# First MLP product of a two-layer trunk kernel by one level of Strassen's algorithm

## The chip, the cores and the metric

The kernel runs on one core of a Trainium2 chip. The metric is the device time of one execution in microseconds. The core has a matrix engine (TensorE, PE in the profile; its weight loads are shown apart as PEld), a vector engine (VectorE, DVE), an engine for activations and copies (ScalarE, ACT), GpSimd (POOL), and SyncE (SP), whose queue issues most of the weight loads by DMA.

## The reference

A trunk of two layers over 512 latent tokens and 256 context tokens of width 1024. Each layer ends with a squared-ReLU MLP. In the names of the kernel:

```
u  = modulate(rms_norm(x), shift, scale)   # 1024 features of each token
ff = u @ w_ff1                             # 1024 x 4096
h  = relu(ff) ** 2
x  = x + gate * (h @ w_ff2)                # 4096 x 1024
```

`shift`, `scale` and `gate` belong to six modulation vectors of each layer, which come from the conditioning vector (latent tokens) or from a learned constant (context tokens). Layer 0 computes all 768 tokens. In layer 1 the result needs the 512 latent ones alone behind the attention stage, so its MLP has 512 tokens. All arithmetic is float32.

## The kernel before, in words

**Numbers.** A float32 product is made of three passes (`PASSES`): each operand is kept as a rounded part and a residue (`uh`/`ul` for the input, `whi`/`wlo` for weights, `hh`/`hl` for the hidden values), and hi·hi, hi·lo and lo·hi are added in PSUM. A weight block of 512 KB comes by DMA into a buffer with the tag `raw` (three of them); ACT casts the rounded part (L158) and DVE subtracts it for the residue (L159), in `split_raw`. Features lie on the 128 partitions, so the 1024 inputs are 8 slices and the 4096 hidden features are 32 chunks of 128; tokens run along the free dimension.

**The MLP** (`mlp`, L1072). The 32 chunks are 8 groups of 4. `ff1(f)` computes the chunks of group f: `dense` (L180, matmul L186) runs 8 slices by 3 passes, each as one matmul of 512 latent columns and, in layer 0, one of 256 context columns, because a matmul writes at most 512 columns here. `act2` (L1075) squares the relu on ACT, rounds it on DVE (L1081) and subtracts for the residue (L1082). The first three chunks of a layer are computed by `First` (L440), slice by slice, as the normalised input becomes ready. `ff2(f)` (L1096) adds the group's part of the second product for the 8 output slices and puts it on x with DVE (`gated_add`, L408). The order is ff1(0), ff1(1), ff2(0), ff1(2), ff2(1) and so on.

**Modulation vectors.** Vectors 0 and 1 of layer 0 are computed at the start, vectors 2 to 4 by `mod_vec` (L242) as matmuls on PE in the attention stage of layer 0. Vector 5 of layer 0 and all six of layer 1 are dot products on DVE beside layer 0's stages up to the end of its MLP (`mod_dot`, L280; L289 is the product, with the weight block, named modw, in a `raw` buffer too).

**What sets the order.** The program is written as generators that yield costs; `weave` mixes those that fill (table `PACE`) with the main one, and a scheduler then sets each engine's order of instructions. Tiles come from pools of a few buffers with the same tag (`u`, `z`, `aw`, `lx`, `ls`, `raw`), and whoever wants a buffer waits for its last reader.

## Time and profile before

| | us |
|---|---|
| three runs | 1634.98, 1635.94, 1640.08 (median 1635.94) |
| the profiled execution | 1638.57 |
| its span | 1635.9 |
| PE busy | 1590.0 (97% of the span), 9202 matmuls |
| PEld busy | 1334.4 (82%) |
| DVE busy | 1075.0 (66%) |
| ACT busy | 584.2 (36%) |
| POOL busy | 63.7 (4%) |
| matmuls of `ff` (L186) on the chain that ended last | 51% of the span |

The span runs from the first to the last instruction that the profiler recorded; the execution's own time is 2.7 us longer. In the chain that ended last, PE has 82% of the span, DVE 2%, ACT 1%. The profile's name `ff` stands for the outputs of both MLP products (`ff1` and `ff2` in the program). The MLP of layer 0 runs from about 460 to 960 us, that of layer 1 from about 1283 to 1625. Matmuls are pipelined: the time of one record is longer than the distance between two, so distances are read from starts. The mean granted clock of the execution was 0.986 of full speed.

### The profile page before, as it was taken

How to read it: one execution, taken by the hardware profiler on the slowest of the kernel's cores; microseconds unless marked ns; L12 is line 12 of the kernel's file. 1: busy time of each engine (PE TensorE's matmuls, PEld its weight loads, DVE VectorE, ACT ScalarE, POOL GpSimd, SP SyncE). 2: the span in 40 equal slices, each digit the busy share in tenths (PEclk: the TensorE clock that was granted, in tenths of full speed). 3: DMA queues.
4: the chain of work that ended last, by engine and by line, in shares of the span. 5: the costliest groups of instructions: out<-in, count | busy, mean ns of one | idle time of the engine just before them, and what ended most of it. 6: DMA issues, size and time to landing. Idle time of an engine off the chain costs nothing.

```text
span 1635.9 us, 23128 instructions
## 1 busy us (share of the span) xinstructions
PE 1590.0 (97%) x9202; PEld 1334.4 (82%) x9202; DVE 1075.0 (66%) x2122; ACT 584.2 (36%) x878; POOL 63.7 (4%) x106
## 2 busy tenths in 40 slices
PE   7988999999999999999999998999999999999997
PEld 3666898789888888888888886888789888888887
DVE  3785576876897676666666487966878644444447
ACT  3462223544442212122122146623655422223223
POOL 1201010000000000000000001101000000000000
PEclk8999999999999999999999999999999999999998
DMA  9347220101354343334333231222102322232233
GB/s 314 114 148 226 86 73 33 65 14 63 106 159 140 115 141 116 115 117 128 125 122 116 78 116 40 78 82 78 65 27 90 104 97 96 90 103 91 91 103 103
DMA packets 58587, 170.48 MB, mean 104 GB/s; under 512 B 6720, under 2 KB 19776, under 8 KB 58480
## 3 DMA queue, kind: packets, MB, share of 16 engines
q1 hardware_dynamic: 55216, 161.26, 30.4%
q0 software_dynamic: 2112, 6.70, 1.4%
q8 instruction: 72, 1.18, 0.3%
q10 hardware_dynamic: 1152, 1.05, 0.2%
q14 instruction: 35, 0.29, 0.1%
HBM read 165.44 MB, written 2.15 MB: 102 GB/s over the span
## 4 chain that ended last, share of the span: by engine, by line
PE 82%; DVE 2%; issue 2%; ACT 1%; POOL 0%; DMA 0%; POOLq 0%; DVEq 0%; ACTq 0%
PE ff L186 51%; PE inp L186 6%; PE outp L186 6%; PE first L440 3%; PE py L178 2%; PE S L998 2%; PE kvp L178 2%; PE pT L1020 2%; PE pn L841 1%; PE S L1000 1%; PE S L1002 1%; PE qrp L186 1%; PE sT L818 1%; PE pi L829 1%; PE lrup L608 1%
## 5 line engine op out<-in xcount | busy, mean ns | idle before, releaser
L158 ACT CAST whi<-raw 128x1024 fp32r<-128x1024 f32 x191 | 200.7, 1051 | 716.2 <-PE ff L186 571.4
L159 DVE TENSOR_TENSOR wlo<-raw,whi 128x1024 fp32r<-128x1024 f32 x191 | 233.2, 1221 | 155.8 <-ACT whi L158 151.4
L186 PE MATMUL ff<-hh,whi 128*128 128x512 f32 (+1 forms) x800 | 242.2, 348 | 0.0
L186 PE MATMUL ff<-hl,whi 128*128 128x512 f32 (+1 forms) x800 | 242.0, 348 | 0.0
L186 PE MATMUL ff<-hh,wlo 128*128 128x512 f32 (+1 forms) x800 | 241.9, 348 | 0.0
L289 DVE SCALAR_TENSOR_TENSOR modjunk<-modw,cb 128x512 f32<-128x512 f32 x224 | 154.7, 691 | 108.6 <-DMA modw<-in_w_modT 103.4
L186 PE MATMUL ff<-uh,whi 128*128 128x512 f32 (+1 forms) x696 | 210.9, 357 | 1.0 <-ACT hrelu L1077 1.0
L186 PE MATMUL ff<-uh,wlo 128*128 128x512 f32 (+1 forms) x696 | 210.2, 356 | 0.0
L186 PE MATMUL ff<-ul,whi 128*128 128x512 f32 (+1 forms) x696 | 209.4, 355 | 0.0
L408 DVE SCALAR_TENSOR_TENSOR x<-ff,mod,x 128x256 f32<-128x256 f32 (+1 forms) x200 | 123.1, 639 | 102.6 <-PE ff L186 102.5
L186 PEld LDWEIGHTS ff<-hl,whi 128*128 128x128 f32 x800 | 150.4, 188 | 20.8
L186 PEld LDWEIGHTS ff<-hh,wlo 128*128 128x128 f32 x800 | 150.3, 188 | 20.6
L186 PEld LDWEIGHTS ff<-hh,whi 128*128 128x128 f32 x800 | 150.3, 188 | 20.5
L186 PEld LDWEIGHTS ff<-uh,whi 128*128 128x128 f32 x696 | 130.8, 188 | 21.8 <-ACT hrelu L1077 1.7
L186 PEld LDWEIGHTS ff<-uh,wlo 128*128 128x128 f32 x696 | 131.0, 188 | 20.6 <-DVE wlo L159 0.5
L186 PEld LDWEIGHTS ff<-ul,whi 128*128 128x128 f32 x696 | 130.7, 188 | 20.5
L186 PE MATMUL inp<-uh,whi 128*128 128x256 f32 (+1 forms) x224 | 71.1, 374 | 2.5 <-ACT whi L158 2.5
L186 PE MATMUL inp<-uh,wlo 128*128 128x256 f32 (+1 forms) x224 | 68.3, 362 | 0.6 <-DVE wlo L159 0.6
L186 PE MATMUL inp<-ul,whi 128*128 128x256 f32 (+1 forms) x224 | 68.3, 362 | 0.0
L193 POOL TENSOR_TENSOR rsq<-rsv,nhalf 128x2 f32<-128x2 f32 (+2 forms) x16 | 14.2, 886 | 1295.8 <-DVE rsv L223 1294.4
L178 PE MATMUL kvp<-whi,uh 128*128 128x256 f32 x192 | 60.2, 313 | 4.2 <-ACT sig L613 2.9
L440 PE MATMUL first<-uh,wlo 128*128 128x256 f32 (+3 forms) x192 | 62.4, 328 | 0.6 <-DVE wlo L159 0.6
(316 smaller groups left out, 2766.2 us busy)
## 6 DMA issues: line engine op xcount, KB each, us to landing
raw<-in_w_ff2c SPq DMA_DIRECT2D x72, 512.0 KB, 3.5
raw<-in_w_ff1c SPq DMA_DIRECT2D x64, 512.0 KB, 3.4
modw<-in_w_modT SPq DMA_DIRECT2D x56, 512.0 KB, 3.9
modw<-in_w_mod SPq DMA_DIRECT2D x24, 512.0 KB, 4.2
raw<-in_w_outc SPq DMA_DIRECT2D x24, 512.0 KB, 3.4
raw<-in_w_inc SPq DMA_DIRECT2D x21, 512.0 KB, 3.5
modw<-in_w_mod SPq DMA_DIRECT2D x32, 256.0 KB, 5.2
raw<-in_w_inkv SPq DMA_DIRECT2D x8, 512.0 KB, 3.5
```

The lines of the kernel that those rows point to most:

```text
L158: nc.scalar.copy(hi, raw)
L159: V.tensor_tensor(lo, raw, hi.bitcast(F32), op=OP.subtract)
L178: mm(dst, w[a], r[b], start=first and i == 0, stop=last and i == 2)
L186: mm(ps[:M, po + t0:po + t1], wk[k][a], rk[k][b][:, t0:t1], start=(k == 0 and i == 0), stop=(k == n - 1 and i == 2))
L289: V.scalar_tensor_tensor(junk, w[:, 512 * i:512 * i + 512], 1.0, rows[2 * r + i], op0=OP.mult, op1=OP.mult, accum_out=acc[:, m, i, r:r + 1])
L408: V.scalar_tensor_tensor(x[m][:, s[0]:s[1]], ps[:, po + s[0]:po + s[1]], modv[l][:, v, m, r:r + 1], x[m][:, s[0]:s[1]], op0=OP.mult, op1=O ...
L440: mm(ps[:M, PO + s[0]:PO + s[1]], wk[k][a][:, :M], self.rk[k][b][:, s[0]:s[1]], start=(k == 0 and i == 0), stop=(k == NK - 1 and i == 2))
L608: mm(ps[:, PO + a:PO + b], wl[:, g, d, c], xs[:, a:b], start=True, stop=True)
L818: mm(sT[h][:, PO + 128 * b:PO + 128 * b + 128], kT[p][hp, bs], z["q"][p][hp, bs], start=True, stop=True)
L829: mm(pi[:, 130 * (b - a):130 * (b - a) + 130], z["q"][p][hp, 128 * b:128 * b + 128], C[p][hp, b], start=True, stop=True)
L998: mm(S[:, PO + a:PO + e], z["qk"][h][wa][:, qs], ckv[ra][:, a:e], start=(i == 0), stop=False)
L1020: nc.tensor.transpose(pt[:, PO + 128 * k:PO + 128 * k + 128], pr[:, 128 * k:128 * k + 128], ident)
```

## The change

The first group of each layer (chunks 0 to 3) is computed as before. The other 28 chunks are taken in 14 pairs. For a pair, the weight is a matrix of 2 by 2 blocks, A11 to A22 (chunk by half of the inputs, that is 4 slices), and the input is one of 2 by 2 blocks, B11 to B22 (half of the inputs by half of the tokens: 384 in layer 0, 256 in layer 1). Strassen's form (Winograd's variant) makes the 2 by 2 output blocks with seven block products in place of eight. A block product is 4 slices by 3 passes, 12 matmuls, all at one line, L1168.

- `combine` (L1106 of the changed file) makes the four input sums for each of 4 slice pairs, once a layer: `u` is put together from its two parts (L1111), four subtractions (L1116), and each result is split into a rounded part (ACT, L1119) and a residue (DVE, L1120).
- `pair` (L1154) makes the weight sums on DVE (L1187, L1188, L1191, L1200), splits each operand of 4 slices (`Halves.of`: ACT L1148, DVE L1149), and adds the products: partly in PSUM, partly through copies by ACT (L1182, L1194, L1198) and additions by DVE (L1185, L1199, L1208). Square and cast of the hidden values are ACT's now (`squares`, L1172 to L1176), the residue is DVE's (L1177).
- The second product is `down` (L1213), with the same matmuls as `ff2` had. The order is written out: four products of a pair, then the second product of the group before in between the last three, then the next pair.
- Vector 5 of layer 0 moves from `mod_dot` to `mod_vec` (PE). `mod_dot` leaves out the context row of vectors 2 to 5 of layer 1, whose context is not needed: 128 products in place of 224.
- `raw` has four buffers in place of three; the cos, sin and mask tables, `nd`, `vw` and `modst` share seven slots of a new tag `t`, and the tables are loaded once a layer; the sums of the inputs take slots `t`, `lx`, `ls` and `z`.

```diff
-        def ff1(f):
-            hs = []
-            if f == 0:
...
-            for i in range(len(hs), FB):
-                w = wchunks(split_raw(ins["w_ff1c"][l, f * FB + i], [128, NK, 128]))
-                ps = ps2("ff1")
-                yield from dense(ps, w, u, segs)
-                hs.append(act2(f, ps))
-            h[f] = hs
...
+        def combine(k, tags):
+
+            sums = []
+            for c in (k, KH + k):
+                t = slot("aw", "usum")
+                V.tensor_tensor(t[:, late], u[c][0][:, late].bitcast(F32), u[c][1][:, late].bitcast(F32), op=OP.add)
+                sums.append(t)
+            a, b = sums
+            for o, i0, i1 in ((a[:, n1], a[:, n2], a[:, n1]), (a[:, n2], b[:, n2], a[:, n2]),
+                              (b[:, n2], b[:, n2], a[:, n1]), (b[:, n1], b[:, n1], b[:, n2])):
+                V.tensor_tensor(o, i0, i1, op=OP.subtract)
+
+            def split(src, hl):
+                nc.scalar.copy(hl[0], src)
+                V.tensor_tensor(hl[1], src, hl[0].bitcast(F32), op=OP.subtract)
+                return hl
+            wide = [slot(next(tags), "t42", F32R) for _ in range(2)]
+            split(b[:, late], [t[:, late] for t in wide])
...
+            split(a[:, n2], t3)
...
+            return lambda: split(a[:, n1], t1)
...
+            def of(self, src):
+                if self.n % 2 == 0:
+                    self.hl = [wp.tile([128, 2, KH, 128], F32R, tag=t, name=t) for t in ("whi", "wlo")]
+                hi, lo = [t[:, self.n % 2] for t in self.hl]
+                self.n += 1
+                nc.scalar.copy(hi, src)
+                V.tensor_tensor(lo, src, hi.bitcast(F32), op=OP.subtract)
+                return hi, lo
...
+            def product(dst, w, name, first, last):
+                hl = halves.of(w)
+                for k in range(KH):
+                    for i, (a, b) in enumerate(PASSES):
+                        mm(dst, hl[a][:, k], right[k][name][b], start=first and k == 0 and i == 0,
+                           stop=last and k == KH - 1 and i == 2, skip_group_check=True)
+                return KH * 1.3e-3 * hN
...
+            def squares(t, done):
+
+                act(t[:, late], t[:, late], AF.Square)
+                hi, lo = slot("z", "hh", F32R), slot("lx" if done % 2 else "ls", "hl", F32R)
+                nc.scalar.copy(hi[:, late], t[:, late])
+                V.tensor_tensor(lo[:, late], t[:, late], hi[:, late].bitcast(F32), op=OP.subtract)
+                return hi, lo
+
+            cost = product(X, a11, "b11", True, False)
+            ta = slot("aw", "hrelu")
+            nc.scalar.copy(ta[:, n1], X)
+            yield cost
+            cost = product(Y, a12, "b21", True, True)
+            V.tensor_tensor(ta[:, n1], ta[:, n1], Y, op=OP.add)
+            s3 = wp.tile([128, KH, 128], F32, tag="s3", bufs=1, name="s3")
+            V.tensor_tensor(s3, a11, a21, op=OP.subtract)
+            V.tensor_tensor(a21, a21, a22, op=OP.add)
+            yield cost
+            cost = product(Z, a21, "t1", True, False)
+            V.tensor_tensor(a11, a21, a11, op=OP.subtract)
+            yield cost
+            cost = product(X, a11, "t2", False, False)
+            nc.scalar.copy(ta[:, n2], X)
+            yield cost
+            cost = product(X, s3, "t3", False, False)
+            tb = slot("aw", "hrelu")
+            nc.scalar.copy(tb[:, n2], X)
+            V.tensor_tensor(tb[:, n2], tb[:, n2], Z, op=OP.add)
+            V.tensor_tensor(a12, a12, a11, op=OP.subtract)
+            yield cost
+            cost = product(X, a22, "t4", False, True)
+            act(tb[:, n2], tb[:, n2], AF.Relu)
+            act(tb[:, n1], X, AF.Relu)
+            h[c + 1] = squares(tb, 1)
+            yield cost
+            cost = product(Z, a12, "b22", False, True)
+            V.tensor_tensor(ta[:, n2], ta[:, n2], Z, op=OP.add)
+            act(ta[:, late], ta[:, late], AF.Relu)
+            h[c] = squares(ta, 0)
+            yield cost
...
+        h = {}
+        tags = iter(TAGS[l])
+        yield from first_group()
+        h.update(enumerate(h.pop(0)))
+        todo = [combine(k, tags) for k in range(KH)]
+        for f in todo:
+            f()
+        G = NF // FB
+        one = pair(FB)
+        yield from steps(one, 4)
+        for f in range(1, G):
+
+            units, two = [], pair(f * FB + 2)
+            g = down(f - 1, [segs], units)
+            for i in range(3):
+                yield from chunks(g, units, i + 1)
+                yield from steps(one, 1)
+            if f < G - 1:
+                yield from chunks(g, units, NK + 1)
+                yield from steps(two, 4)
+                one = pair((f + 1) * FB)
+                for i in range(3):
+                    yield from chain(steps(one, 1), steps(two, 1))
+                yield from steps(one, 1)
...
+        yield from down(G - 1, sweeps, None)
...
-        filler = chain(*[mod_vec(0, v, PACE["mod"][0]) for v in range(2, 5)]) if l == 0 else None
...
+        filler = chain(*[mod_vec(0, v, PACE["mod"][0]) for v in range(2, 6)]) if l == 0 else None
```

**Where the order changes, first place: DVE behind the first group of layer 0's MLP.** Before, DVE has there the casts and residues of the squared chunks (`hh`, `hl`), residues of weights (`wlo`), and modulation products (`modjunk`):

```order
L1081 CAST hh_4294<-hrelu_4291 128x768
L289 SCALAR_TENSOR_TENSOR modjunk_4184,modacc_4232<-modw_4423,cb_4181 128x512
L1082 TENSOR_TENSOR hl_4295<-hrelu_4291,hh_4294 128x768
L1081 CAST hh_4301<-hrelu_4298 128x768
L159 TENSOR_TENSOR wlo_4389<-raw_4386,whi_4388 128x1024
L1082 TENSOR_TENSOR hl_4302<-hrelu_4298,hh_4301 128x768
L1081 CAST hh_4308<-hrelu_4305 128x768
L289 SCALAR_TENSOR_TENSOR modjunk_4184,modacc_4232<-modw_4423,cb_4182 128x512
L1082 TENSOR_TENSOR hl_4309<-hrelu_4305,hh_4308 128x768
L289 SCALAR_TENSOR_TENSOR modjunk_4184,modacc_4232<-modw_4423,cb_4183 128x512
L159 TENSOR_TENSOR wlo_4457<-raw_4454,whi_4456 128x1024
```

Now the sums of the inputs stand there. `usum` is a sum of the two parts of an input slice or a difference of such; `ul`, `t42` and `t3` are residues of the sums; `raw_4511` and `raw_4513` are the two weight blocks of the first pair. The first rows, from the first cast on:

```order
L1084 CAST hh_4356<-hrelu_4353 128x768
L1085 TENSOR_TENSOR hl_4357<-hrelu_4353,hh_4356 128x768
L1084 CAST hh_4363<-hrelu_4360 128x768
L292 SCALAR_TENSOR_TENSOR modjunk_4401,modacc_4293<-modw_4399,cb_4238 128x512
L1085 TENSOR_TENSOR hl_4364<-hrelu_4360,hh_4363 128x768
L1084 CAST hh_4370<-hrelu_4367 128x768
L292 SCALAR_TENSOR_TENSOR modjunk_4401,modacc_4293<-modw_4399,cb_4239 128x512
L1085 TENSOR_TENSOR hl_4371<-hrelu_4367,hh_4370 128x768
L292 SCALAR_TENSOR_TENSOR modjunk_4401,modacc_4293<-modw_4399,cb_4240 128x512
L1149 TENSOR_TENSOR wlo_4518<-raw_4511,whi_4517 128x512
L292 SCALAR_TENSOR_TENSOR modjunk_4401,modacc_4293<-modw_4399,cb_4241 128x512
L1111 TENSOR_TENSOR usum_4443<-uh_3962,ul_3963 128x768
```

and the last ones ahead of the weight of the third product (`wlo_4561`), with those just behind it:

```order
L1120 TENSOR_TENSOR t3_4486<-usum_4489,t3_4485 128x384
L1116 TENSOR_TENSOR usum_4491<-usum_4491 128x384
L292 SCALAR_TENSOR_TENSOR modjunk_4537,modacc_4293<-modw_4535,cb_4238 128x512
L1149 TENSOR_TENSOR wlo_4561<-raw_4513,whi_4560 128x512
L1120 TENSOR_TENSOR t42_4498<-usum_4491,t42_4497 128x768
L292 SCALAR_TENSOR_TENSOR modjunk_4537,modacc_4293<-modw_4535,cb_4239 128x512
L1185 TENSOR_TENSOR hrelu_4533<-hrelu_4533,str_4515 128x384
L292 SCALAR_TENSOR_TENSOR modjunk_4537,modacc_4293<-modw_4535,cb_4240 128x512
L1191 TENSOR_TENSOR raw_4511<-raw_4513,raw_4511 128x512
L292 SCALAR_TENSOR_TENSOR modjunk_4537,modacc_4293<-modw_4535,cb_4241 128x512
L159 TENSOR_TENSOR wlo_4595<-raw_4592,whi_4594 128x1024
```

Between these two pieces are 35 more rows, nearly all of `combine`; the residue of the third product's weight is the 51st operation from the cast `hh_4356` on.

**Second place: PE at the same point.** Before, the matmuls of one chunk follow those of another, with the same inputs:

```order
L186 MATMUL ff1_4318<-ul_3919,whi_4314 128x256
L186 MATMUL ff1_4318<-ul_3919,whi_4314 128x512
L186 MATMUL ff1_4318<-uh_3918,wlo_4315 128x256
L186 MATMUL ff1_4318<-uh_3918,wlo_4315 128x512
L186 MATMUL ff1_4392<-uh_3904,whi_4388 128x256
L186 MATMUL ff1_4392<-uh_3904,whi_4388 128x512
L186 MATMUL ff1_4392<-ul_3905,whi_4388 128x256
L186 MATMUL ff1_4392<-ul_3905,whi_4388 128x512
```

Now the first two products of the pair write `str_4515`; behind the first one, the start of the third (`strq_4516`, with `whi_4560`) and eight matmuls of the second MLP product are put:

```order
L1168 MATMUL str_4515<-uh_3968,wlo_4518 128x384
L1168 MATMUL strq_4516<-uh_3962,whi_4560 128x384
L186 MATMUL ff2_4598<-hh_4356,whi_4594 128x256
L186 MATMUL ff2_4598<-hh_4356,whi_4594 128x512
L186 MATMUL ff2_4598<-hl_4357,whi_4594 128x256
L186 MATMUL ff2_4598<-hl_4357,whi_4594 128x512
L186 MATMUL ff2_4632<-hh_4356,whi_4594 128x256
L186 MATMUL ff2_4632<-hh_4356,whi_4594 128x512
L186 MATMUL ff2_4632<-hl_4357,whi_4594 128x256
L186 MATMUL ff2_4632<-hl_4357,whi_4594 128x512
L1168 MATMUL strq_4516<-ul_3963,whi_4560 128x384
L1168 MATMUL str_4515<-uh_3970,whi_4517 128x384
```

and behind the second product the rest of the third, which reads `ul_3963` and `wlo_4561` (the residues in the lists of DVE above) and is followed by all others of the pair:

```order
L1168 MATMUL str_4515<-uh_3976,wlo_4518 128x384
L1168 MATMUL strq_4516<-uh_3962,wlo_4561 128x384
L1168 MATMUL strq_4516<-uh_3964,whi_4560 128x384
L1168 MATMUL strq_4516<-ul_3965,whi_4560 128x384
L1168 MATMUL strq_4516<-uh_3964,wlo_4561 128x384
```

The third product reads the tile of slice 0 whose second half of tokens DVE and ACT have written over with a sum.

**Third place: the head of a later group in layer 0.** SP's queue of loads there (modw: modulation weights; `in_w_ff1c` and `in_w_ff2c`: weights of the two MLP products), before:

```order
L155 DMA raw_5067<-in_w_ff1c 128x1024
L286 DMA modw_5092<-in_w_modT 128x1024
L155 DMA raw_5135<-in_w_ff1c 128x1024
L286 DMA modw_5160<-in_w_modT 128x1024
L155 DMA raw_5203<-in_w_ff2c 128x1024
L155 DMA raw_5265<-in_w_ff2c 128x1024
L286 DMA modw_5285<-in_w_modT 128x1024
```

and now; `raw_5733` is the first weight block of the second product in its group, and its buffer is the one that `modw_5647` had:

```order
L1159 DMA raw_5587<-in_w_ff1c 128x1024
L1159 DMA raw_5589<-in_w_ff1c 128x1024
L288 DMA modw_5647<-in_w_modT 128x1024
L288 DMA modw_5728<-in_w_modT 128x1024
L155 DMA raw_5733<-in_w_ff2c 128x1024
L288 DMA modw_5773<-in_w_modT 128x1024
L155 DMA raw_5818<-in_w_ff2c 128x1024
```

DVE at that place now (`hrelu` additions are those of product results, `hl` residues of hidden values):

```order
L1199 TENSOR_TENSOR hrelu_5625<-hrelu_5625,strq_5512 128x384
L1185 TENSOR_TENSOR hrelu_5607<-hrelu_5607,str_5591 128x384
L1177 TENSOR_TENSOR hl_5672<-hrelu_5625,hh_5671 128x768
L292 SCALAR_TENSOR_TENSOR modjunk_5649,modacc_5581<-modw_5647,cb_4238 128x512
L292 SCALAR_TENSOR_TENSOR modjunk_5649,modacc_5581<-modw_5647,cb_4239 128x512
L1208 TENSOR_TENSOR hrelu_5527<-hrelu_5527,strq_5512 128x384
L292 SCALAR_TENSOR_TENSOR modjunk_5730,modacc_5581<-modw_5728,cb_4238 128x512
L292 SCALAR_TENSOR_TENSOR modjunk_5730,modacc_5581<-modw_5728,cb_4239 128x512
L1177 TENSOR_TENSOR hl_5710<-hrelu_5527,hh_5709 128x768
L159 TENSOR_TENSOR wlo_5736<-raw_5733,whi_5735 128x1024
```

Before, the loads of the second product came one behind another, and each pair of modulation products stood between splits; now a modulation load comes ahead of the first of them, and its two products stand behind the residue `hl_5672`, ahead of `wlo_5736`.

## Rows read from the trace of the kernel before

**Rows 1.** Windows: stretch, length, busy us (count) of PE, PEld, DVE, ACT, POOL, clock, DMA, GB/s.
```profile
460.00:960.00 500.00, 499.77 (x2879) 437.86 (x2878) 338.53 (x702) 121.05 (x139) 0.66 (x1) 1.00 0.38 125
1283.00:1625.00 342.00, 340.93 (x1568) 280.66 (x1568) 167.85 (x221) 108.09 (x144) 0.70 (x1) 1.00 0.30 98
```

**Rows 2.** Timeline of PE, layer 0's MLP; columns: start, us, instruction; eleven passes apart.
```profile
599.88 0.51 PE L186 MATMUL ff<-hh,wlo 128*128 128x256 f32 x2
...
603.71 0.51 PE L186 MATMUL ff<-ul,whi 128*128 128x256 f32 x2
```

**Rows 3.** Timeline of PE, layer 1's MLP, eighteen matmuls apart.
```profile
1399.67 0.39 PE L186 MATMUL ff<-uh,wlo 128*128 128x512 f32 x1
...
1403.84 0.39 PE L186 MATMUL ff<-hh,wlo 128*128 128x512 f32 x1
```

**Rows 4.** Timeline of PE, last second product of layer 1, 73 matmuls apart.
```profile
1600.39 0.28 PE L186 MATMUL ff<-hh,whi 128*128 128x256 f32 x1
...
1609.06 0.29 PE L186 MATMUL ff<-hl,whi 128*128 128x256 f32 x1
```

**Rows 5.** Groups by form, PE: busy us, mean ns, idle before.
```profile
L186 PE MATMUL ff<-hh,whi 128*128 128x512 f32 x480 | 188.9, 394 | 0.0
...
L186 PE MATMUL ff<-hh,whi 128*128 128x256 f32 x320 | 89.6, 280 | 0.0
```

**Rows 6.** Groups by form, DVE.
```profile
L289 DVE SCALAR_TENSOR_TENSOR modjunk<-modw,cb 128x512 f32<-128x512 f32 x224 | 154.7, 691 | 108.6 <-DMA modw<-in_w_modT 103.4
...
L1082 DVE TENSOR_TENSOR hl<-hrelu,hh 128x768 fp32r<-128x768 f32 x32 | 30.6, 957 | 0.8
...
L1082 DVE TENSOR_TENSOR hl<-hrelu,hh 128x512 fp32r<-128x512 f32 x32 | 22.2, 693 | 1.1
...
L213 DVE TENSOR_TENSOR n1acc<-n1acc,n1sq 128x256 f32<-128x256 f32 x21 | 8.8, 418 | 0.1
```

**Rows 7.** Timeline of DVE ahead of and behind the first group of layer 0.
```profile
442.75 0.74 DVE L337 SCALAR_TENSOR_TENSOR xn<-x,mod,nps 128x512 f32<-128x512 f32 x1
...
445.40 2.06 DVE L337 SCALAR_TENSOR_TENSOR xn<-x,mod,nps 128x512 f32<-128x512 f32 x3
...
462.10 0.56 DVE L1081 CAST hh<-hrelu 128x768 fp32r<-128x768 f32 x1
```

**Rows 8.** Timeline of ACT at the end of chunk 3, layers 0 and 1; idle before.
```profile
469.38 0.81 ACT L1077 ACTIVATE hrelu<-ff 128x768 f32<-128x768 f32 x1 [3.27 <-PE ff L186]
...
1289.50 1.05 ACT L158 CAST whi<-raw 128x1024 fp32r<-128x1024 f32 x1 [1.56 <-PE ff L186]
```

**Rows 9.** Timeline of DVE, first cast of layer 1's MLP.
```profile
1284.56 0.43 DVE L1081 CAST hh<-hrelu 128x512 fp32r<-128x512 f32 x1 [0.28 <-ACT hrelu L1078]
```

**Rows 10.** Windows of 1 and 2 us where PE was idle.
```profile
102.00:103.00 1.00, 0.27 (x3) 0.07 (x1) 1.00 (x1) 0.00 (x0) 0.00 (x0) 1.00 0.07 29
...
106.00:107.00 1.00, 0.74 (x6) 0.41 (x10) 1.00 (x4) 0.00 (x0) 0.00 (x0) 0.50 0.00 0
...
110.00:111.00 1.00, 1.00 (x9) 0.20 (x8) 0.57 (x2) 0.81 (x3) 0.00 (x0) 0.50 0.71 287
...
1148.00:1150.00 2.00, 0.61 (x4) 0.18 (x3) 1.91 (x4) 1.97 (x3) 0.00 (x0) 1.00 0.00 0
```

**Rows 11.** Groups by form, ACT.
```profile
L158 ACT CAST whi<-raw 128x1024 fp32r<-128x1024 f32 x191 | 200.7, 1051 | 716.2 <-PE ff L186 571.4 <-PE inp L186 55.4 <-DMA raw<-in_w_inc 22.2
...
L1025 ACT CAST pTh<-pT 128x384 fp32r<-128x384 f32 x64 | 30.6, 478 | 37.3 <-PE pT L1020 26.7 <-DVE pTl L1026 10.2
...
L1078 ACT ACTIVATE hrelu<-hrelu 128x768 f32<-128x768 f32 x32 | 27.0, 848 | 0.9
```

**Rows 12.** DMA issues: KB each, median us from issue to landing.
```profile
raw<-in_w_ff2c SPq DMA_DIRECT2D x72, 512.0 KB, 3.5
```

**Rows 13.** Groups by form, PE's matmuls of the modulation vectors.
```profile
L249 PE MATMUL modp<-modw,cs 128*32 128x256 f32 x192 | 17.1, 432 | 0.3 <-DMA modw<-in_w_mod 0.3
```

**Rows 14.** Window of 1 us in the stage of the modulation loads.
```profile
142.00:143.00 1.00, 0.69 (x6) 0.49 (x5) 0.93 (x4) 0.00 (x0) 0.00 (x0) 1.00 1.00 324
```

More of the change, by code (lines that the diff above doesn't have):

```diff
@@ L461, in in_gates @@
         else:
-            raw, hi, lo = [[wp.tile([128, NK, 128], dt, tag=t, bufs=3, name=t) for _ in range(3)]
+            raw, hi, lo = [[wp.tile([128, NK, 128], dt, tag=t, bufs=NRAW if t == "raw" else 3, name=t) for _ in range(3)]
                            for t, dt in (("raw", F32), ("whi", F32R), ("wlo", F32R))]
@@ L1098, in ff2, with first_group @@
-        def ff2(f):
+        hN = (T - t0) // 2
+        n1, n2 = slice(t0, t0 + hN), slice(t0 + hN, T)
+        late = slice(t0, T)
+        def first_group():
+            first = First([wchunks(split_raw(ins["w_ff1c"][l, i], [128, NK, 128])) for i in range(3)], u, [128] * 3)
+            yield from mod.finish(first)
+            h[0] = [act2(i, ps) for i, ps in enumerate(first.ps)]
+            w = wchunks(split_raw(ins["w_ff1c"][l, 3], [128, NK, 128]))
+            ps = ps2("ff1")
+            yield from dense(ps, w, u, segs)
+            h[0].append(act2(3, ps))
@@ new lines, in mlp, with __init__ @@
+        class Halves:
+            def __init__(self):
+                self.n = 0
+            def of(self, src):
[6 more added lines that the diff above has]
+                return hi, lo
+        halves = Halves()
@@ new lines, in pair @@
+        def pair(c):
+            raws = []
+            for i in range(2):
+                raws.append(wp.tile([128, 2, KH, 128], F32, tag="raw", bufs=NRAW, name="raw"))
+                dma(raws[i], ins["w_ff1c"][l, c + i].rearrange("p (h k) m -> p h k m", h=2))
+            (a11, a12), (a21, a22) = [[r[:, 0], r[:, 1]] for r in raws]
+            p, q = ps2("str"), ps1("strq")
+            X, Y, Z = p[:, :hN], p[:, 512:512 + hN], q[:, :hN]
+            def product(dst, w, name, first, last):
[43 more added lines that the diff above has]
+            yield cost
@@ L1105, in ff2 @@
                         ps = ps2("ff2")
-                        yield from dense(ps, [(w[0][:, mi, i], w[1][:, mi, i]) for i in range(FB)], h[f], sg)
+                        order = (0, 1, 3, 2)
+                        yield from dense(ps, [(w[0][:, mi, i], w[1][:, mi, i]) for i in order],
+                                         [h[f * FB + i] for i in order], sg)
                         gated_add(l, 5, m, ps, sg)
@@ L1111, in ff2, with steps, chunks @@
                             norm.add(x[m], sg)
-        h = {}
-        yield from ff1(0)
-        for f in range(1, NF // FB):
-            yield from ff1(f)
-            yield from ff2(f - 1)
-            del h[f - 1]
-        yield from ff2(NF // FB - 1)
+                        if units is not None:
+                            units.append(m)
+        def steps(g, n):
+            for _ in range(n):
+                yield next(g)
+        def chunks(g, units, n):
+            while len(units) < n and (c := next(g, None)) is not None:
+                yield c
+        h = {}
+        tags = iter(TAGS[l])
[20 more added lines that the diff above has]
+                yield from steps(one, 1)
+            else:
+                yield from steps(two, 4)
+                for i in range(3):
+                    yield from chain(chunks(g, units, 4 + i), steps(two, 1))
+                yield from chunks(g, units, NK + 1)
+            for i in range(FB):
+                del h[(f - 1) * FB + i]
+        yield from down(G - 1, sweeps, None)
     tags = iter(["z"] * 13 + ["ls"] * 4 + ["lx"] * 2 + ["z"] * 13)
@@ L1196, in trunk_kernel @@
             rows = []
-            filler = chain(mod_rows(rows), mod_dot(0, 5, PACE["dot5"][0], rows), *[mod_dot(1, v, PACE["dot"][0], rows) for v in range(6)])
+            filler = chain(mod_rows(rows), *[mod_dot(1, v, PACE["dot"][0], rows) for v in range(6)])
         else:
```

97 lines of the change are left out of this document (56 added, 41 removed).

## Prediction

> **What bounds the kernel now.** I read three views first. The windows of the two MLP stages [rows 1] show TensorE (PE) busy for 499.77 of 500 us in layer 0 and 340.93 of 342 in layer 1, at full granted clock; VectorE (DVE) has 338.5 and 167.9, ScalarE (ACT) 121 and 108. So both stages are bound by the matmul stream, and a matmul saved there is time saved, as long as the other engines feed it. Then the timeline of PE, for the distance between starts, since durations overlap: a weight pass over 768 tokens (one matmul of 256 columns and one of 512) starts every (603.71 − 599.88) / 11 = 0.348 us [rows 2], one of 512 columns every (1403.84 − 1399.67) / 18 = 0.2317 us [rows 3], one of 256 every (1609.06 − 1600.39) / 73 = 0.1188 us [rows 4], each with its own weight load. The price is thus about proportional to columns; the busy means of the grouped view (394 and 280 ns, [rows 5]) are not prices. Last I read how long each DVE form takes [rows 6], because the change puts new DVE work ahead of the matmuls.
>
> **The saving.** Chunks 4 to 31 of each layer become 14 pairs. A pair was 2 chunks × 8 slices × 3 passes = 48 weight passes; it becomes 7 products × 4 slices × 3 = 84 matmuls over half the tokens. Layer 0: 48 × 0.348 = 16.70 against 84 matmuls of 384 columns, which the trace lacks; halfway between 0.1188 and 0.2317 is 0.175, half of 0.348 is 0.174, so 84 × 0.175 = 14.70. Saved 2.00 a pair, **−28.0** for 14. Layer 1: 48 × 0.2317 = 11.12 against 84 × 0.1188 = 9.98, 1.14 a pair, **−16.0**. A column costs 0.453, 0.453 and 0.464 ns by the three distances [rows 2 to 4]; so I hold each term to 3 us if starts go by columns, and if they don't, that is rival E.
>
> **The setup in layer 0.** Sums of the input halves must stand before the third product. In the new order DVE does, from the first squared chunk (hh_4356) to the residue of the third product's weight (wlo_4561 from raw_4513), 51 operations: 4 casts 768 wide (0.56 each), 15 operations 768 wide (0.957), 24 of 384 (0.556, halfway between those of 256 and 512), 3 of 512 (0.693) and 5 modulation products (0.69) [rows 6, 7]: 35.5 us; back-to-back records overlap (one of 0.74 us, and three in 2.06 [rows 7]), about 0.07 each, so 31.9. DVE comes to the first cast at 462.1 [rows 7], hence 494.0. PE ends chunk 3 at 469.4, when ACT's relu starts [rows 8]. In the 24.6 us between it has products 1 and 2 (24 × 0.175 = 4.2), two more matmuls and eight of the second MLP product (1.4 + 0.35): 5.95. Idle 18.7; another 7 DVE operations up to wlo_4595 (5.0) against 2.1 of PE work give 2.9. Term **+21.6**. Before, the same place had no hole, since DVE did only casts, residues and weight splits there. If ACT's copies between the sums (one behind each DVE result) come late it is more; if the records overlap more, or fewer operations lie ahead of the third product, less: bounds 10 and 30.
>
> **The setup in layer 1.** From DVE's first cast at 1284.56 [rows 9] there are 46 operations up to the same point: 4 × 0.43 + 21 × 0.693 + 21 of 256 columns × 0.418 [rows 6, 9] = 25.05, less 45 × 0.07 = 21.9, so 1306.5. Chunk 3 ends at 1289.5, where ACT waited for it [rows 8]; PE has 3.55 us of the 17.0, so 13.4 idle, and 0.6 behind it: **+14.0** (bounds 8 and 18).
>
> **The clock behind these holes.** PE was idle from 102.3 to 106.3; the granted clock fell to 0.50 (1.2 GHz) during that hole and stayed there until 111, some 5 us after PE began again, while an idle of 1.4 us in 1148 to 1150 left it at 1.00 [rows 10]. Two holes of 13 to 20 us therefore cost 5 us at half speed each, 2.5 lost: **+5.0** (bounds 0 and 10).
>
> **The heads of the groups.** From the second group on, PE runs 11 products in a row, 23.1 us, before the second MLP product of the group ahead, whose first weight load reuses a raw buffer. In the new order that buffer is given free by two modulation products that stand behind the last residue of the first pair on DVE. Product 6 ends at 16.8; relu (384 columns, about 0.48), square (0.848) and cast (0.83, between rows) on ACT [rows 11] and the residue (0.957) on DVE bring 20.1; two modulation products (0.69) 21.5; the load 3.5 [rows 12]: 25.0; ACT's split 1.05 [rows 11]: 26.1. PE waits 3.0. In the first such group one more addition and four products stand there, 5.4. Of the six heads in layer 0 two have the buffer free early; four pay 3 × 3.0 + 5.4 = **+14.4** (bounds 0, if the scheduler's order lets DVE run ahead of PE, and 24, six heads at 4).
>
> **One more modulation vector.** The fifth moves from DVE, beside layer 0's MLP, to PE, in the stage before. PE spends 17.1 us on three now [rows 13], so **+5.7** if PE is full there; 2 if much of it falls into idle places; if its eight loads (4.19 MB) can't go beside others at the 324 GB/s that was reached [rows 14], 12.9. Both layers' MLP lose 96 of 224 modulation products on DVE (−66 us) and gain some 81 in the pairs' additions and splits and 22 in the setup: 338.5 becomes about 375 of 500, so DVE is no bound on average, and costs only where stated. ACT takes copies from 121 to roughly 200 of 500, nothing. The smaller table tiles, the fourth raw buffer and the constants loaded twice lie beside PE work of the attention stages; I take 0 (bounds −2 and 3).
>
> **Sum.** −28.0 − 16.0 + 21.6 + 14.0 + 5.0 + 14.4 + 5.7 = +16.7. The profiled execution took 1638.57 us, so 1655.3; it stands 2.6 above the median 1635.94, so **1653** against the median.
>
> A page speaks against the saving itself. The Trainium skill, "TensorE: Matmul & The Clock Gate", section "Back-to-back issue gap", gives a sustained spacing of about 81 ns at 128 columns and 131 at 512, mostly a fixed price. By estimate from it 256 columns cost 98 and 384 cost 114, and the 28 pairs would lose some 8 us instead of gaining 44. The trace disagrees: 0.2317 against 0.1188 [rows 3, 4], a ratio of 1.95.
>
> **Rivals.**
> B, faster. The holes at the heads vanish (DVE is ahead of PE there, or the buffer falls free earlier), the vector fits in idle PE time, and the clock recovers at once: −44.0 + 35.6 = −8.4, so 1630 against the profiled execution and **1628**. For it: all three costs rest on an order, not on a row that shows the wait, and the heads are wrong if one release is wrong. Against: the slow clock behind the 4 us hole [rows 10]. If the setups too are half as long, 1610.
> D, no change. The heads vanish, vector and clock are paid: −44.0 + 35.6 + 5.0 + 5.7 = +2.3, **1638**.
> C, slower still. The clock also falls at the heads, 2.5 × 4 = 10, and the loads of the modulation vector are limited by the DMA (+7): **1663** to 1670. For it: the fall after a hole of 4 us; against, the hole of 1.4 us that left the clock alone [rows 10].
> The same page's section on HAM oscillation says that repeated idle gaps re-throttle the engine each time; no row here shows gaps at such a spacing.
> E. A matmul has a fixed price, and busy means are the price: a pair of layer 0 would go from 48 × (0.394 + 0.280) = 32.4 to 84 × 0.337 = 28.3 us, one of layer 1 from 48 × 0.394 = 18.9 to 84 × 0.280 = 23.5; 14 × (4.6 − 4.1) = +8 in place of −44: **1705**. The distances speak against it [rows 2 to 4].
>
> **How the numbers follow.** Forecast 0.42 (its own range 1643 to 1663, from the bounds of the setups and heads), B 0.30, D 0.14, C 0.11, E 0.03. About 0.3% (5 us) is what a measurement of this kernel can tell from no change, so the forecast, C and E are slower: 0.56; D is the same: 0.14; B faster: 0.30. The range takes in D, most of B and most of C: 1620 to 1668.
>
> **What would show it.** Right: in each MLP, behind the first group, PE holes of about 19 and 13 us ended by DVE's residues (the new lines L1120 and L1149); matmuls of L1168 0.175 and 0.119 us apart; holes of 3 to 5 us where the first `ff2` matmul of a group waits for ACT's split of a late load; clock 0.50 for some 5 us behind the long ones; stage before the MLP 5 to 6 us longer; layer 0's MLP about 510 us, layer 1's about 342. Wrong: holes under 8 us in both setups (then B), no waits at the heads (D or B), starts further apart than columns say (E).

## The result, and the profile after

The changed kernel takes 1653.61 us (median of 4 runs, 1651.96 to 1657.16) against 1635.46 for the kernel before: ratio 1.0108, 95% interval 1.0083 to 1.0133. It is slower by 1.1%, and the forecast of 1653 with a range of 1620 to 1668 holds. The profiled execution took 1653.95 us, its span 16.0 us more than that of before; by the medians the difference is 18.2, because the profiled execution of before (1638.57) stood 3.1 us above its median and this one 0.3. The first lines of the page:

```profile
span 1651.9 us, 24459 instructions
...
PE 1566.6 (95%) x9604; PEld 1357.3 (82%) x9604; DVE 1179.7 (71%) x2284; ACT 727.2 (44%) x1210; POOL 63.6 (4%) x105
```

PE is busy for 23 us less than before, so the matmuls were saved, and yet the span is longer. Where that comes from is read by stage. Windows of the kernel before, cut at PE's first matmul of chunk 3 in each layer and at the first matmul of the norm behind layer 0's MLP (columns as in rows 1; the first row is all that lies ahead of layer 0's chunk 3):

```profile
0.00:460.69 460.69, 435.84 (x2753) 347.70 (x2753) 313.43 (x680) 195.44 (x326) 36.93 (x60) 0.96 0.36 112
...
460.69:958.24 497.55, 497.55 (x2868) 436.63 (x2869) 336.86 (x699) 119.72 (x137) 0.00 (x0) 1.00 0.38 124
1283.57:1635.90 352.33, 342.75 (x1576) 282.10 (x1576) 172.00 (x233) 107.93 (x143) 1.39 (x2) 0.99 0.30 99
```

The same three stretches of the changed kernel:

```profile
0.00:461.37 461.37, 437.99 (x2818) 346.89 (x2818) 310.16 (x669) 195.95 (x326) 36.83 (x60) 0.99 0.38 120
...
461.37:972.12 510.75, 479.87 (x2701) 441.93 (x2701) 364.83 (x696) 198.19 (x305) 0.23 (x3) 0.97 0.35 116
1296.14:1651.88 355.74, 336.14 (x2080) 300.04 (x2080) 251.00 (x407) 172.18 (x309) 1.39 (x2) 0.97 0.29 97
```

Layer 0's MLP grew by 13.2 us, layer 1's with the end of the program by 3.4; the stretch ahead by 0.7; what lies between (325.3, now 324.0) shrank by 1.3. Length less PE's busy time is its idle time: 30.9 us more in layer 0, 10.0 more in layer 1. The timeline of PE shows where, with what ended each idle time:

```profile
473.50 0.45 PE L1168 MATMUL strq<-uh,whi 128*128 128x384 f32 x1 [1.29 <-ACT uh L1119]
...
491.25 0.69 PE L1168 MATMUL str<-uh,whi 128*128 128x384 f32 x1 [13.52 <-ACT hrelu L1182]
...
567.54 1.00 PE L186 MATMUL ff<-hh,whi 128*128 128x256 f32 x2 [4.85 <-ACT whi L158]
...
635.45 0.69 PE L186 MATMUL ff<-hh,whi 128*128 128x256 f32 x2 [3.17 <-ACT whi L158]
...
766.18 1.01 PE L186 MATMUL ff<-hh,whi 128*128 128x256 f32 x2 [3.08 <-ACT whi L158]
...
835.16 0.62 PE L186 MATMUL ff<-hh,whi 128*128 128x256 f32 x2 [3.00 <-ACT whi L158]
...
1308.68 0.58 PE L1168 MATMUL strq<-ul,whi 128*128 128x256 f32 x1 [2.39 <-DVE ul L1120]
...
1313.10 0.58 PE L1168 MATMUL strq<-ul,whi 128*128 128x256 f32 x1 [3.41 <-DVE ul L1120]
...
1317.96 0.58 PE L1168 MATMUL strq<-uh,whi 128*128 128x256 f32 x1 [3.42 <-ACT uh L1119]
```

One long hole in layer 0 and several in layer 1 lie behind the first groups, and four waits of 3.00 to 4.85 us (14.1 together) lie at heads of groups in layer 0. At most of them the clock fell. These windows are the five stretches of the two MLPs in which the granted clock was at its lower level, 0.50 (1.2 GHz); one more, in the last 9 us of the program, both kernels have:

```profile
475.40:495.90 20.50, 6.65 (x21) 5.65 (x20) 20.50 (x38) 7.86 (x14) 0.00 (x0) 0.50 0.00 0
567.60:571.00 3.40, 3.40 (x11) 2.89 (x12) 3.00 (x5) 0.93 (x2) 0.00 (x0) 0.50 0.85 234
635.90:639.30 3.40, 3.40 (x12) 2.88 (x11) 3.13 (x7) 0.53 (x2) 0.00 (x0) 0.51 0.49 146
765.60:772.40 6.80, 6.22 (x20) 5.36 (x21) 4.04 (x8) 1.57 (x3) 0.00 (x0) 0.50 0.56 197
1308.30:1321.90 13.60, 6.34 (x24) 5.46 (x25) 13.54 (x30) 5.27 (x13) 0.00 (x0) 0.50 0.00 0
```

PE was busy for 26.0 us of these, and half of that, 13.0 us, is what the low clock cost: 9.8 in layer 0, 3.2 in layer 1. In the two long windows DVE was busy for 20.50 of 20.50 and 13.54 of 13.60 us.

The distance between matmuls went by columns. In layer 0 nine starts of 384 columns take (706.91 − 705.35) / 9 = 0.173 us, in layer 1 56 starts of 256 columns (1406.50 − 1399.78) / 56 = 0.120 (timeline of PE):

```profile
705.35 0.51 PE L1168 MATMUL str<-t,whi 128*128 128x384 f32 x2
...
706.91 0.51 PE L1168 MATMUL str<-t,whi 128*128 128x384 f32 x2
...
1399.78 0.28 PE L1168 MATMUL str<-uh,whi 128*128 128x256 f32 x1
...
1406.50 0.28 PE L1168 MATMUL strq<-uh,wlo 128*128 128x256 f32 x1
```

Set beside the prediction, in us of the span:

| term | forecast | measured | how |
|---|---|---|---|
| saving, layer 0 | −28.0 | −27.5 | 13.2 − 30.9 − 9.8 |
| saving, layer 1 | −16.0 | −9.8 | 3.4 − 10.0 − 3.2 |
| hole at the sums, layer 0 | +21.6 | +16.8 | 30.9 − 14.1 |
| holes at the sums, layer 1 | +14.0 | +10.0 | windows |
| waits at the heads | +14.4 | +14.1 | four rows |
| half clock | +5.0 | +13.0 | five windows |
| modulation vector, rest of the change | +5.7 | +0.7 − 1.3 | stages |
| sum | +16.7 | +16.0 | |

The sum was met more closely than its terms. The experiments ask which of these are causes.

### The profile page after: what moved, and what is told of

It reads as the page before. It is cut to its first block, busy times and chain, and to the rows that moved or that the text cites. A ratio compares the mean times of both kernels' runs of the same rounds, so it can differ in the third digit from the quotient of the medians.

```text
span 1651.9 us, 24459 instructions
## 1 busy us (share of the span) xinstructions
PE 1566.6 (95%) x9604; PEld 1357.3 (82%) x9604; DVE 1179.7 (71%) x2284; ACT 727.2 (44%) x1210; POOL 63.6 (4%) x105
## 4 chain that ended last, share of the span: by engine, by line
PE 76%; DVE 5%; issue 3%; ACT 2%; DMA 1%; POOL 0%; POOLq 0%; DVEq 0%; ACTq 0%
PE ff L186 28%; PE str L1168 14%; PE outp L186 6%; PE inp L186 6%; PE strq L1168 5%; PE py L178 2%; PE first L443 2%; PE S L1001 2%; PE kvp L178 2%; PE pT L1023 1%; PE pn L844 1%; DMA raw<-in_w_ff2c 1%; DVE usum L1116 1%; PE S L1005 1%; PE S L1003 1%
## 5 line engine op out<-in xcount | busy, mean ns | idle before, releaser
L411 DVE SCALAR_TENSOR_TENSOR x<-ff,mod,x 128x256 f32<-128x256 f32 (+1 forms) x200 | 123.4, 640 | 96.3 <-PE ff L186 96.2
L1148 ACT CAST whi<-raw 128x512 fp32r<-128x512 f32 x168 | 100.5, 620 | 191.0 <-PE ff L186 118.3
L1168 PE MATMUL str<-t,whi 128*128 128x384 f32 (+1 forms) x560 | 127.3, 315 | 0.6 <-ACT whi L1148 0.6
L1149 DVE TENSOR_TENSOR wlo<-raw,whi 128x512 fp32r<-128x512 f32 x168 | 112.1, 686 | 16.3 <-ACT whi L1148 15.4
L1168 PE MATMUL str<-uh,whi 128*128 128x256 f32 (+1 forms) x280 | 88.2, 315 | 13.6 <-ACT hrelu L1182 13.5
L1168 PEld LDWEIGHTS str<-t,whi 128*128 128x128 f32 x560 | 96.1, 189 | 2.7 <-ACT whi L1148 0.9
L1168 PE MATMUL str<-t,wlo 128*128 128x384 f32 (+1 forms) x280 | 88.0, 314 | 0.0
L1168 PE MATMUL str<-ul,whi 128*128 128x256 f32 (+1 forms) x280 | 86.3, 308 | 0.0
L1168 PE MATMUL str<-uh,wlo 128*128 128x256 f32 (+1 forms) x280 | 86.3, 308 | 0.0
L1177 DVE TENSOR_TENSOR hl<-hrelu,hh 128x768 fp32r<-128x768 f32 (+1 forms) x56 | 46.0, 821 | 44.3 <-ACT hh L1176 44.1
L1168 PE MATMUL strq<-ul,whi 128*128 128x384 f32 (+1 forms) x224 | 70.3, 314 | 6.1 <-DVE ul L1120 6.1
L1168 PE MATMUL strq<-uh,whi 128*128 128x384 f32 (+1 forms) x224 | 70.1, 313 | 6.0 <-ACT uh L1119 6.0
```

The source lines that it names most:

```text
L411: V.scalar_tensor_tensor(x[m][:, s[0]:s[1]], ps[:, po + s[0]:po + s[1]], modv[l][:, v, m, r:r + 1], x[m][:, s[0]:s[1]], op0=OP.mult, op1=O ...
L1148: nc.scalar.copy(hi, src)
L1149: V.tensor_tensor(lo, src, hi.bitcast(F32), op=OP.subtract)
L1168: mm(dst, hl[a][:, k], right[k][name][b], start=first and k == 0 and i == 0, stop=last and k == KH - 1 and i == 2, skip_group_check=True)
L1177: V.tensor_tensor(lo[:, late], t[:, late], hi[:, late].bitcast(F32), op=OP.subtract)
```

## Experiments

Each version was timed beside the kernel before on the same chip, and each ratio is to that; the medians of the kernel before were 1635.06, 1636.89 and 1634.22 us on the three occasions.

**1. The heads of the groups.** Here the last three products of the second pair go between units of the second MLP product (a unit is one of its 8 output slices) in every group, as the change has it in its last group alone:

```diff
+            yield from steps(two, 4)
+            for i in range(3):
+                yield from chain(chunks(g, units, 4 + i), steps(two, 1))
+            yield from chunks(g, units, NK + 1)
             if f < G - 1:
-                yield from chunks(g, units, NK + 1)
-                yield from steps(two, 4)
                 one = pair((f + 1) * FB)
-                for i in range(3):
-                    yield from chain(steps(one, 1), steps(two, 1))
-                yield from steps(one, 1)
+                yield from steps(one, 4)
...
```

> The changed kernel with one order altered: in every group the second pair's last three products are set between units of the second MLP product, as the change does in its last group alone, in place of eleven products in a row. Theory: the four waits of 3.0 to 4.9 us in layer 0 (14.1 us) go, since the last hidden values are ready and the raw buffer is free long before the next group's second product, and with them three stretches at the half clock behind them (about 6 us): 1653.6 - 20 = 1634 us. Rival: the four raw buffers are the limit whatever the order, since two pairs and the second product's blocks share them; the waits move to other places of the group and the time stays within 1648 to 1658.

Measured: 1633.31 us, ratio to before 0.9995 (0.9976 to 1.0014). The four waits are gone and with them the low clock there; the window of layer 0's MLP:

```profile
459.19:950.67 491.48, 474.06 (x2701) 437.30 (x2701) 362.13 (x696) 199.31 (x305) 0.23 (x3) 0.98 0.37 121
```

It is 19.3 us shorter than with the change, close to 14.1 + 6.5. So the heads cost what the prediction said, and the clock behind them as much as half of that again. What holds the buffer was tried next, by leaving the modulation products out.

```diff
+        V.memset(acc, 0.0)
         for m in range(NK):
-            w = wp.tile([128, D], F32, tag="raw", bufs=NRAW, name="modw")
-            dma(w, ins["w_modT"][6 * l + v - NMR, m])
-            junk = slot("aw", "modjunk", shape=[512])
-            for r in conds:
...
             yield pace
```

> The changed kernel without the modulation products on DVE and their loads: layer 1's modulation vectors hold their biases alone. Theory: the buffer that the first block of a group's second product waits for is held by these products; without them the four waits in layer 0 (14.1 us) and the half clock behind them (about 6 us) go, and the hole at the sums is shorter by five products (3 us): 1628 to 1634 us. Rival: eleven products in a row hold all raw buffers whatever else is loaded; waits of 2 us and more stay at the heads: 1640 and above.

Measured: 1629.20 us, and no wait at any head; layer 0's MLP takes 488.0 us:

```profile
458.31:946.33 488.02, 474.04 (x2701) 438.55 (x2702) 284.94 (x434) 197.25 (x305) 0.23 (x3) 0.98 0.22 71
```

The rival (the buffers are short whatever is loaded) falls. This version takes the products' time off DVE as well as their loads out of the buffers; that it is the buffer is shown by the course in the changed kernel (timeline, second of the four heads), which is that of the prediction: a residue of hidden values, two modulation products, the load (SPq is SP's queue), its split, and the matmul at 635.45. DVE had been idle for 3.80 us ahead of the residue, and the load goes out as the second product ends. In layer 1's MLP, beside which no modulation products run, no head waited.

```profile
628.33 0.96 DVE L1177 TENSOR_TENSOR hl<-hrelu,hh 128x768 fp32r<-128x768 f32 x1 [3.80 <-ACT hh L1176]
629.32 0.69 DVE L292 SCALAR_TENSOR_TENSOR modjunk<-modw,cb 128x512 f32<-128x512 f32 x1
...
630.06 0.69 DVE L292 SCALAR_TENSOR_TENSOR modjunk<-modw,cb 128x512 f32<-128x512 f32 x1
...
630.78 0.33 SPq L155 DMA_DIRECT2D raw<-in_w_ff2c  x1
...
634.35 1.04 ACT L158 CAST whi<-raw 128x1024 fp32r<-128x1024 f32 x1 [0.27 <-DMA raw<-in_w_ff2c]
```

**2. The sums of the inputs.** First without them:

```diff
-        todo = [combine(k, tags) for k in range(KH)]
-        for f in todo:
-            f()
+        for k in range(KH):
+            b11, b21, b22 = [t[:, n1] for t in u[k]], [t[:, n1] for t in u[KH + k]], [t[:, n2] for t in u[KH + k]]
+            b12 = [t[:, n2] for t in u[k]]
+            right[k] = {"b11": b11, "b21": b21, "b22": b22, "t1": b12, "t2": b11, "t3": b12, "t4": b21}
```

> The changed kernel without the sums of the inputs: products 3 to 6 of each pair read blocks of the input instead, so the hidden values are other ones; the sums of weights and results stay. Theory: the holes behind the first groups are the time that DVE needs for the sums: idle 16.8 and 10.5 us go, with some 6 us lost at half clock behind them: 1653.6 - 33 = about 1620 us. Rival: half of the holes is the rest of DVE's backlog there (casts, residues, modulation products), which stays: about 1637.

Measured: 1618.93 us, 0.989 of before (0.9846 to 0.9934). Both holes are gone, the heads' waits stay, and the saving shows. The holes with their clock are thus worth 34.7 us, and the rest of DVE's backlog, the rival, leaves no wait over 1.5 us there. The version leaves out DVE's part of the sums together with ACT's casts and the buffers of both, so by itself it does not tell these apart.

Then work was put over the hole: the second product of the first group ahead of the first pair.

```diff
+        yield from down(0, [segs], [])
         one = pair(FB)
...
-            g = down(f - 1, [segs], units)
+            g = down(f - 1, [segs], units) if f > 1 else iter(())
```

> The changed kernel with the second product of the first group put ahead of the first pair, so that PE has 33.4 us of work in layer 0 and 22 in layer 1 while DVE makes the sums of the inputs. Theory: the holes are DVE work that PE waits for; DVE has about 32 + 5 + 8 us (layer 0) and 22 + 5 + 6 (layer 1) to do, so holes of 5 to 8 us and 2 to 5 stay of 16.8 and 11.3, and part of the half clock behind them: 1635 to 1642 us. Rival: the work that is moved ahead is missing where it stood (between the last products of the first two pairs), and PE waits there for the same time: 1650 to 1656.

Measured: 1648.93 us, a miss for both theories: in layer 1 one hole of 8.6 us took the place of several, in layer 0 15.2 and 3.2 us took the place of 16.8. The timeline of PE and DVE there says why:

```profile
479.37 0.47 DVE L411 SCALAR_TENSOR_TENSOR x<-ff,mod,x 128x256 f32<-128x256 f32 x1
...
495.29 0.73 DVE L411 SCALAR_TENSOR_TENSOR x<-ff,mod,x 128x512 f32<-128x512 f32 x1
...
496.08 1.01 PE L186 MATMUL ff<-hh,whi 128*128 128x256 f32 x2 [15.23 <-DVE x L411]
```

The covering matmuls write PSUM, which DVE's additions to x (L411, `gated_add`) free, and these stood behind the sums in DVE's order; the two halves of one addition are 16 us apart, with one modulation product and otherwise sums and splits between them. So PE waited for DVE all the same, one step further on. Together with the order of experiment 1:

> Both alterations of the two kernels ahead of this one together. Theory: the gains add: 14.1 us of waits and 6 of half clock at the heads, 12 to 18 us at the sums: 1614 to 1624 us, under the 1635.5 of the kernel before. Rival: the two gains are the same one (DVE's backlog), then no better than the better of the two, about 1634.

Measured: 1631.14 us, 0.9974 (0.9957 to 0.9991): 2.2 us better than the new order of the heads alone, which the spread of the two (1629.02 to 1634.58 and 1628.76 to 1640.67) does not tell from nothing. The two did not add as expected, since the cover gave so little.

**3. A version that beats both.** The order of experiment 1 stays, the sums go between the units that cover them, and the modulation products pause meanwhile (a cost of 0 holds back the work that is woven in):

```diff
...
+        g = down(0, [segs], units)
+        for k in range(KH):
+            for _ in chunks(g, units, 2 * k + 1):
+                yield 0.0
+            todo.append(combine(k, tags))
+            for _ in chunks(g, units, 2 * k + 2):
+                yield 0.0
...
```

> The two alterations together, with the sums of the inputs set between the units of the second product that covers them (so that the additions to x that free PSUM are not queued behind all sums on DVE), and with no modulation products meanwhile. In the kernel with both alterations PE still stood 18.5 us in layer 0 and 8.6 in layer 1, waiting for these additions. Theory: DVE has some 43 us to do in layer 0 against 38 of PE, 27 against 25 in layer 1, so holes of 5 and 3 us stay: 1631.1 - 18 to 20, with less half clock, 1608 to 1615 us. Rival: the wait for the sums comes back at the third product of the first pair at full length, and the time stays at 1626 to 1632.

Measured: 1612.36 us (1608.32 to 1615.02), ratio to before 0.984 (0.9802 to 0.9878): some 41 us under the change, 1.6% faster than before. Its two MLP stages, and PE's longest holes left there:

```profile
460.60:937.40 476.80, 470.81 (x2700) 434.35 (x2701) 364.30 (x698) 197.85 (x305) 0.23 (x3) 1.00 0.39 124
1266.60:1613.20 346.60, 333.82 (x2080) 298.71 (x2080) 251.78 (x409) 173.08 (x309) 1.39 (x2) 0.99 0.30 99
```

```profile
506.29 0.44 PE L1168 MATMUL str<-uh,wlo 128*128 128x384 f32 x1 [2.87 <-DVE wlo L1149]
...
1297.79 0.39 PE L1168 MATMUL str<-uh,wlo 128*128 128x256 f32 x1 [2.64 <-DVE wlo L1149]
```

What is new here, interleaving and pause, wasn't tried apart; but beside layer 1's MLP no modulation products run that could pause, and there the hole went from 8.6 us to 2.64 by the interleaving alone. Idle in layer 0 is 6.0 us now, at full clock, and 497.6 − 476.8 + 6.0 = 26.8 is again the saving of layer 0.

**4. The rest of the change.** The vector moved alone, in the kernel before, with the rates (`PACE`) at which the change weaves in the modulation work:

```diff
-NMR = 5
+NMR = 6
...
-        filler = chain(*[mod_vec(0, v, PACE["mod"][0]) for v in range(2, 5)]) if l == 0 else None
+        filler = chain(*[mod_vec(0, v, PACE["mod"][0]) for v in range(2, 6)]) if l == 0 else None
```

> The kernel before with the change to the modulation vectors alone: vector 5 of layer 0 on PE in the attention stage, no context row for vectors 2 to 5 of layer 1, the MLP as it was. In the trace of the change the MLP of layer 0 begins only 0.7 us later than before, though 5.7 us of matmuls were added. Theory: the added matmuls fall into places where PE was idle, so this kernel takes 1633 to 1638 us, no change. Rival: they cost their 5.7 us, and in the changed kernel fewer stretches at the half clock in the first 300 us paid it back by chance; then 1640 to 1642.

Measured: 1642.72 us, 1.0045 (1.0029 to 1.006): the rival's price. That is 7.7 us (4.7 to 9.8 by the interval): the vector costs what the prediction said, or a little more, though the trace of the change had suggested that it was free. Then everything of the change but Strassen's products:

```diff
+        if True:
+            yield from plain()
+            return
+
         h = {}
```

(`plain` is the loop of the kernel before, `ff1` and `ff2`.)

> The changed kernel with the first MLP product as it was before in both layers; all else of the change stays (modulation vector on PE, four raw buffers, tables in shared slots). In the trace of the change the MLP of layer 0 begins at 461.4 us, with the modulation vector moved alone at 467.0, before at 460.7. Theory: the fourth raw buffer (and the slots) gave back in the attention stage what the vector cost; this kernel takes 1634 to 1639 us, the MLPs 497.5 and 352.4 as before. Rival: the early start in the changed kernel was the clock's luck; then it takes 1640 to 1645, as the kernel with the vector moved alone (1642.7).

Measured: 1634.27 us, 0.9988 (0.9967 to 1.0008). Something in the rest pays the vector back. The fourth raw buffer was the suspect, so the same kernel was run with three (`NRAW` 3 for 4) beside one with four:

> The changed kernel with the first MLP product as before in both layers (1634.3 us with four raw buffers), and with three raw buffers: the modulation vector on PE and the tables in shared slots stay. Theory: the fourth raw buffer lets the loads of the modulation weights go earlier beside others and takes 4 to 7 us of PE's idle and half-clock time out of the attention stage; with three the kernel takes 1640 to 1643 us, as with the vector moved alone (1642.7), and the MLP of layer 0 begins near 466. Rival: the slots, the order or chance did it; then it stays at 1633 to 1637.

> The same kernel with four raw buffers once more, on the same chip as the one with three, so that the two are compared directly: 1633 to 1637 us under either theory.

Measured: 1640.24 us with three buffers, 1633.35 with four, on the same chip, twelve executions each (1633.71 to 1645.35 and 1630.06 to 1638.09): the fourth buffer is worth some 6.9 us. The stretch ahead of layer 0's chunk 3, with three and then with four:

```profile
0.00:469.53 469.53, 442.17 (x2818) 348.75 (x2818) 309.29 (x667) 196.67 (x327) 36.67 (x59) 0.97 0.38 118
```

```profile
0.00:462.17 462.17, 439.07 (x2818) 348.12 (x2818) 309.03 (x667) 196.04 (x326) 36.81 (x60) 0.98 0.38 121
```

In these two executions (5.1 and 1.9 us above their medians) the same matmuls take 7.4 us longer; 4.3 of that is more idle time of PE, 3.1 more busy time at a lower mean clock.

## Why the prediction was right, and where its terms were not

**What bounds the kernel** was right: PE, with prices by columns [rows 2 to 4]. Rival E falls: 0.173 and 0.120 us were measured where it needed 0.337 and 0.280, and with most of the holes gone (experiment 3) the change gains in both layers. The estimate by the spacing in the Trainium skill, "TensorE: Matmul & The Clock Gate", section "Back-to-back issue gap", falls too: it needed 0.114 and 0.098.

**The saving of layer 0** was right. **That of layer 1** was mis-sized, 9.8 for 16.0. Starts 0.120 apart instead of 0.1188 make a pair's gain 1.04 for 1.14 us, 14.6 for 14; and from the end of the low clock (1321.9) on, 41 starts, at or just behind changes between products or to another width, come 0.04 to 0.11 us late, 3.4 us together, as here, 0.33 instead of 0.23 us apart (timeline of PE). That leaves 11.2; the other 1.4 us stay open.

```profile
1410.87 0.50 PE L186 MATMUL ff<-hh,whi 128*128 128x512 f32 x1
1411.20 0.28 PE L1168 MATMUL str<-uh,whi 128*128 128x256 f32 x1
```

**The setup** was right in its cause and in DVE's part: the residue of the third product's weight, put at 494.0, ran at 493.51 to 494.19. The forecast hole was 4.8 us too long because of PE's part: the second product, counted as done early, ran only at 491.25, at the end of the hole. It waited for ACT's copy of the first product:

```profile
490.72 0.48 ACT L1182 COPY hrelu<-str 128x384 f32<-128x384 f32 x1 [0.41 <-DVE t L1120]
```

That copy stands behind casts of the sums in ACT's order and was released by DVE. It writes into a tile of the tag `aw`, as the sums do, and there are three of these; that it waited for such a tile is argued from the names, and wasn't tried apart. The product ran at half clock, and so filled 4 us that the forecast had put down as idle. In layer 1, which began 12.6 us later than before, the forecast end of DVE's work (1306.5) becomes 1319.1, and the last of the sums ran there (timeline of DVE):

```profile
1319.33 0.42 DVE L1116 TENSOR_TENSOR usum<-usum 128x256 f32<-128x256 f32 x1
```

The hole there was 4.0 us too long in the forecast, and came in pieces, because PE did matmuls between the sums, at half clock, which took 3.2 us more than at full.

**The heads** were right in place, mechanism and size (14.1 for 14.4; the first 4.85 for 5.4, the others 3.00 to 3.17 for 3.0), and experiment 1 shows the cause. One name was wrong: the residue ahead of the modulation products is not the last of its pair but the first of two (the other ran at 634.11), as the timing in the prediction has it.

**The clock** was the term that failed most, 13.0 for 5.0. At the sums it was 6.5, by (6.65 + 6.34) / 2: the clock was low not only behind the holes, as forecast, but from 475.4 on in layer 0, 2.3 us before the long hole began at 477.7 (PE had been idle for 1.29 us shortly before), and between the holes of layer 1. There hole and clock are not two causes, since DVE was behind all the time; together they came to 33.3 us (34.7 in experiment 2) against a forecast of 40.6. The heads cost another 6.5, by (3.40 + 3.40 + 6.22) / 2, which the forecast had at nothing. This is rival C's mechanism, given 0.11 beside the forecast as if one excluded the other, while [rows 10] had no hole between 1.4 and 4 us to decide by. The Trainium skill, "TensorE: Matmul & The Clock Gate", section "HAM oscillation", says that repeated idle gaps re-throttle the engine; this trace agrees for three of the four waits (at those of 4.85, 3.17 and 3.08 us the clock went to 0.50, at the one of 3.00 no low stretch is seen).

**The vector** cost 7.7 us alone, and the 5.7 lies within its interval. The step that failed is the one that put the fourth raw buffer at 0: it was worth some 6.9 us, outside the bound of −2 that was set. The two nearly cancel, but the +0.7 of the stretch is theirs only in part. The stretches at low clock ahead of layer 0's chunk 3, added up (windows; five of 6.8 us before, then four of 3.4 us with the change):

```profile
sum 34.13, PE 30.86 PEld 17.64 DVE 19.12 ACT 13.24 POOL 5.55; mean PE 6.17 PEld 3.53 DVE 3.82 ACT 2.65 POOL 1.11
```

```profile
sum 13.66, PE 13.23 PEld 7.59 DVE 9.83 ACT 5.70 POOL 1.19; mean PE 3.31 PEld 1.90 DVE 2.46 ACT 1.43 POOL 0.30
```

Half of PE's time in them, 15.4 and 6.6 us, was lost there. How much of this difference the buffer made, and how much the one execution of before that was profiled, 3.1 us above its median, isn't known.

So the total was within 1 us by luck, because errors cancelled: +8.0 for the clock and +6.2 for layer 1's saving against −8.8 for the holes and −6.3 for buffer and stages. Taken with their clock, the setups came out 7.3 us under the forecast and the heads 6.2 us over.

## What to carry to other kernels

A saving on the bound engine can be lost whole until the work that prepares it has cover: here 31 us of PE time in layer 0 went to sums on DVE and, in four groups, to a load whose buffer was held by work woven in beside it, and most of it came back when the order alone was changed. Cover must not itself need the engine that it hides: put the preparation between the covering units, so that what frees their buffers is not queued behind it. And price the small companions of a change one by one: a vector at about +7.7 and a buffer at about −6.9 look like nothing together.
